# Two parts of down ahead of the first chunk in seven products, and the last half tile of the output in two pieces

## The chip, the cores and the metric

The kernel runs on one core of one Trainium2 chip. Its time is the device time of one execution in microseconds (us). Three runs of the kernel before took 1874.52 to 1875.6 us, with a median of 1874.64.

The engines are TensorE (PE; its weight loads are listed apart as PEld), VectorE (DVE), ScalarE (ACT), GpSimd (POOL) and SyncE (SP), which here issues the DMAs.

## The reference

A decoder of two layers on a sequence of 512 tokens of width 1024. Each layer has a feed-forward network (FFN), a mixer and another FFN, each behind an RMSNorm and added to x:

```python
def rmsnorm(x, g):
    y = x * lax.rsqrt(jnp.mean(x * x, axis=-1, keepdims=True) + EPS)
    return y * g

def swiglu(h, w_gate, w_up, w_down):
    return (jax.nn.silu(h @ w_gate) * (h @ w_up)) @ w_down

for i in range(2):
    x = x + 0.5 * swiglu(rmsnorm(x, ffn1_norm[i]), ffn1_w_gate[i], ...)
    x = x + mixer(rmsnorm(x, mix_norm[i]))     # i = 0: gated linear attention, i = 1: stick-breaking
    x = x + 0.5 * swiglu(rmsnorm(x, ffn2_norm[i]), ffn2_w_gate[i], ...)
return rmsnorm(x, final_norm)
```

w_gate and w_up are 1024 x 2816, w_down is 2816 x 1024, all float32. The change touches the four FFNs and the final norm; the mixers stay as they are.

## The kernel before, in words

**Split operands.** x lives in SBUF as eight tiles `xs[k]` of 128 features by 512 tokens, float32. TensorE multiplies in a float32 form with fewer bits, so each operand is cut into a high part (a cast) and a low part (operand minus high part), and each product is three matmuls: high by high, low by high, high by low (`mm3`, L67). For a weight, `Entry.split` (L108) does it: ScalarE casts (L124), VectorE subtracts (L126). Tiles `wh` and `wl` hold 1024 columns each and have four buffers; half-wide ones, `vh` and `vl`, have one. The loads themselves, issued by SyncE at L89, go to `raw` (1 MB of gate or up, two buffers) or `rawd` (512 KB of down, two buffers).

**The feed.** All of TensorE's work on weights stands in one list of entries, each with its weights and a body that issues its matmuls. When an entry starts (`Feed.start`, L137 on), the weights of up to three entries from it on are split, as long as no more than four units are needed, those up to four are viewed (a view may itself compute a sum of weights), and those up to six are loaded. The order of the entries is the order on TensorE. On the other engines a scheduler places the instructions after a model of their times, so one that is written later may stand earlier.

**An FFN** (class `FFN`). The 2816 hidden features are eleven chunks of 256 in six groups: chunks 0-1, 2-3, 4-5, 6-7, 8 and 9-10. For chunks 0 and 1, each half chunk of gate and of up is a feature entry (`feat`): 24 matmuls of 512 columns. The first six features take the input not yet normalized, while four pieces of `normed_input` (L615 among their lines) prepare the normalized one.

From chunk 2 on, gate and up come by `seven`: a 2 x 2 block product made from seven products instead of eight, by sums of weights (`s12`, `s34`; L506 to L513) and sums of inputs (`ts`, cut by L605 and L606 into `th` and `tl`). One chunk of gate or up is two entries. `body_1` has four of the products, `body_2` three; each is 12 matmuls of 256 columns at L523. `body_1` copies its first product to a second PSUM bank (L547) before its third product goes into the first bank. `body_2` begins with a product of the `s34` weights. Its results go through VectorE (L566, L569) and the gate (SiLU at L533, or the multiply at L536), and for an up chunk through `close`, which cuts the hidden features into `hh` and `hl`.

The eight cut sums of the input come from `sums`. The first five are spread over the entries that lie between the sixth and number `sums_by` of the FFN, the number at which the first chunk in seven products begins.

**Down** (L292). A group of four hidden features is multiplied by w_down in four parts, one entry each: two tiles of 128 output features, each 4 x 3 matmuls of 512 columns into one PSUM bank, then one VectorE operation that adds half of it to `xs[k]` (L307). The parts of a group's down are put between the entries of the next group. In entry order, with S for a chunk in seven products (two entries), g and u for gate and up and d0 to d3 for the parts of down of chunks 0 and 1:

```
8 features, S g2, d0, S u2, d1, S g3, d2, S u3, d3, S g4, ...
```

**The end.** In the last FFN, the last group's down is `back_tok` (L316): tokens on the partitions, 512 of the 1024 features in each of eight half tiles (i = 0..3 tokens, dh = 0, 1), 4 x 3 matmuls of 512 columns each. `last` (L1198) then adds half of it to x (L1201), squares and sums it (L1204), and for dh = 0 multiplies by the norm's gain (L1207). For dh = 1 it adds the two halves' sums (L1210), takes `rstd` (L377 to L388, seven small operations), scales both halves (L1212, L1214) and issues the two output DMAs (L1213, L1215).

Of the kernel before, what the change touches and what calls it, by code (L numbers as in the profile page):

```python
# [10 lines left out]
F32 = mybir.dt.float32  # L11
# [3 lines left out]
AF = mybir.ActivationFunctionType  # L15
ALU = mybir.AluOpType
PSUM = bass.MemoryType.PSUM

P = 128
T = 512  # L20
D = 1024
KD = D // P
FF = 2816
NT = T // P
EPS = 1e-6
# [7 lines left out]
def decoder(ctx: ExitStack, tc: tile.TileContext, a: dict, out: bass.AP):  # L33
    nc = tc.nc
# [6 lines left out]
    sp = ctx.enter_context(tc.tile_pool(name="sp", bufs=1))  # L41
# [5 lines left out]
    def psum(name, tag=None):  # L47
        if tag is None:
            tag = order[turn_[0] % 8]
            turn_[0] += 1  # L50
        return pp.tile([P, T], F32, tag=tag, bufs=banks[tag], name=name)
# [5 lines left out]
    gT = cp.tile([P, 51], F32, name="gT")  # L57
# [5 lines left out]
    def mm(ps, l, r, first, last):  # L63
        st["pe"] = nc.tensor.matmul(ps, l, r, start=first, stop=last).ins  # L64

    def mm3(ps, wh, wl, mh, ml, first, last):
        mm(ps, wh, mh, first, False)  # L67
        mm(ps, wl, mh, False, False)
        mm(ps, wh, ml, False, last)
# [219 lines left out]

                feed.q.append(Entry([u], body))  # L290

    def down(w, r0, nf, hs, part, nxt):  # L292

        nd = KD // nf
        src = w[r0 : r0 + nf * P, part * nd * P : (part + 1) * nd * P]
        ch = Chunk(src.rearrange("(f p) c -> p f c", p=P), nf, nd * P)
        ch.few = True

        def body(W):
            (wh, wl), = W  # L300
            for m in range(nd):
                ps = psum("ps_d")
                s = slice(m * P, (m + 1) * P)
                for f in range(nf):
                    mm3(ps, wh[:, f, s], wl[:, f, s], hs[f][0], hs[f][1], f == 0, f == nf - 1)
                k = part * nd + m
                nc.vector.scalar_tensor_tensor(  # L307
                    out=xs[k], in0=ps, scalar=0.5, in1=xs[k], op0=ALU.mult, op1=ALU.add
                )
                if nxt is not None:  # L310
                    nxt(k)
                yield

        feed.q.append(Entry([(ch, lambda t: t, nf, nd * P)], body))

    def back_tok(w, r0, nf, hs, done):  # L316

        units = []
        for dh in range(2):
            src = w[r0 : r0 + nf * P, dh * 512 : dh * 512 + 512]  # L320
            ch = Chunk(src.rearrange("(f p) c -> p f c", p=P), nf, 512)
            for u in range(0, nf, 2):
                units.append((ch, (lambda t, u=u: t[:, u : u + 2]), 2, 512))

        def body(W):
            for i in range(NT):
                s = slice(i * P, (i + 1) * P)
                for dh in range(2):
                    ps = psum("ps_bt")
                    for f in range(nf):  # L330
                        wh, wl = W[dh * (nf // 2) + f // 2]
                        hh, hl = hs[f]
                        mm(ps, hh[:, s], wh[:, f % 2], f == 0, False)
                        mm(ps, hh[:, s], wl[:, f % 2], False, False)
                        mm(ps, hl[:, s], wh[:, f % 2], False, f == nf - 1)
                    done(dh, i, ps)
            yield

        feed.q.append(Entry(units, body))


    st = {}
# [23 lines left out]
    def stats_a(tag=None):  # L366

        if st["ss"] is None:
            sums = st["sums"]
        else:  # L370
            ps = psum("ps_st", tag)
            for i in range(NT):
                mm(ps[:, i : i + 1], st["ss"][:, i * P : (i + 1) * P], ones[:, 0:1], True, True)
            sums = ps[:, 0:NT]
        st["r4"] = rstd(sums, NT)

    def rstd(sums, n):  # L377
        v = sp.tile([P, n], F32, tag="rv", bufs=2, name="rv")
# [56 lines left out]
    class FFN:  # L435
# [4 lines left out]


        GROUPS = ((0, 2), (2, 4), (4, 6), (6, 8), (8, 9), (9, 11))
        NORMED, SEVEN = 6, 2
        SEVEN_UP = (2, 3, 4, 5, 6, 7, 8, 9, 10)

        def __init__(self, wg, wu, wd, gi, nxt, first=False, last=False):
            self.gi, self.normed = gi, False
            self.defer, self.gates = [], []
            self.lead = []
            self.hs = [[] for _ in self.GROUPS]  # L450
            base, downs = len(feed.q), []
            self.sums_by = 10**6
            for group, (c0, c1) in enumerate(self.GROUPS):
                slots, put = 2 * (c1 - c0), 0
                for i in range(slots):
                    c, f = c0 + i // 2, i % 2
                    if f == 0:
                        g, u = Chunk(cols(wg, c * 256, 256), KD, 256), Chunk(cols(wu, c * 256, 256), KD, 256)
                    d = self.defer if i == 0 and c == 0 else None
                    f_ = f  # L460
                    if first and c == 0:

                        g, u = (Chunk(cols(w, f * P, P), KD, P) for w in (wg, wu))
                        self.lead += [g, u]
                        f_ = 0
                    if c >= self.SEVEN:
                        if f == 0:
                            self.sums_by = min(self.sums_by, len(feed.q) - base)
                            self.seven(g)
                    elif c not in self.SEVEN_UP:  # L470
                        feat(g, f_, self.evac_g, defer=d)
                    elif f == 0:
                        feat(g, 0, self.evac_g), feat(g, 1, self.evac_g)
                        self.sums_by = min(self.sums_by, len(feed.q) - base)
                    if c not in self.SEVEN_UP:
                        feat(u, f_, lambda ps, h=group: self.evac_u(ps, h), defer=d)
                    elif f == 1:
                        self.seven(u, group)

                    while c >= self.SEVEN and put < len(downs) * (i + 1) // slots:  # L480
                        down(*downs[put])
                        put += 1
                for x in downs[put:]:
                    down(*x)
                n = 2 * (c1 - c0)
                end = group + 1 == len(self.GROUPS)
                downs = [(wd, c0 * 256, n, self.hs[group], part, nxt if end else None) for part in range(n)]
            self.count = len(feed.q) - base
            if last:
                back_tok(wd, c0 * 256, n, self.hs[group], nxt)  # L490
            else:
                for x in downs:
                    down(*x)
            self.total = len(feed.q) - base
# [686 lines left out]
    xt = {}  # L1181

    def to_tokens(tp):
        fin = st["fin"] = tp.tile([P, D], F32, tag="s", bufs=4, name="fin")
        nc.gpsimd.dma_start(fin, a["final_norm"].partition_broadcast(P))

        for hf in range(2):
            ps = [psum("ps_T") for _ in range(NT)]
            for m in range(4):
                for i in range(NT):  # L1190
                    nc.tensor.transpose(
                        ps[i][:, m * P : (m + 1) * P], xs[hf * 4 + m][:, i * P : (i + 1) * P], ident
                    )
            for i in range(NT):
                xt[i, hf] = xs[hf * 4 + i]
                nc.scalar.copy(xt[i, hf], ps[i])

    def last(dh, i, ps):  # L1198

        x = xt[i, dh]  # L1200
        nc.vector.scalar_tensor_tensor(out=x, in0=ps, scalar=0.5, in1=x, op0=ALU.mult, op1=ALU.add)  # L1201
        fin = st["fin"]
        sq = st["sq"][:, 2 * i + dh : 2 * i + dh + 1]
        nc.scalar.activation(ps, x, AF.Square, accum_out=sq)  # L1204
        rows = out[0, i * P : (i + 1) * P]
        if dh == 0:
            nc.vector.tensor_tensor(out=x, in0=x, in1=fin[:, 0:T], op=ALU.mult)  # L1207
            return
        s = st["sq"][:, 2 * i : 2 * i + 1]
        nc.vector.tensor_tensor(out=s, in0=s, in1=sq, op=ALU.add)  # L1210
        r = rstd(s, 1)
        nc.vector.scalar_tensor_tensor(out=x, in0=x, scalar=r, in1=fin[:, T:D], op0=ALU.mult, op1=ALU.mult)  # L1212
        nc.sync.dma_start(rows[:, T:D], x)  # L1213
        nc.scalar.activation(xt[i, 0], xt[i, 0], AF.Copy, scale=r)  # L1214
        nc.sync.dma_start(rows[:, 0:T], xt[i, 0])  # L1215

    ffn(1, 0, 0, lambda k: prep(k, 2), first=True)
    phases.append(
# [9 lines left out]
    with tc.tile_pool(name="ip", bufs=1) as ip:  # L1228
# [9 lines left out]
        sums = [ip.tile([P, NT], F32, name=f"sums{hf}") for hf in range(2)]  # L1238
# [8 lines left out]
        ps = psum("ps_g")  # L1247
# [34 lines left out]
    for ph in phases[:-1]:  # L1282
        ph.run()

    st["sq"] = gT[:, 0 : 2 * NT]
    phases[-1].run(between=to_tokens)


# [38 lines left out]
```

## Time and profile before

| what | value |
|---|---|
| median of three runs | 1874.64 us |
| the profiled execution | 1874.33 us |
| its span, first to last instruction | 1872.2 us |
| TensorE busy | 1847.3 us, 99% of the span |
| VectorE busy | 1412.0 us, 75% |
| ScalarE busy | 1012.5 us, 54% |
| DMA | 95 GB/s over the span |
| last matmul starts / span ends | 1864.08 / 1872.2 us |

A line of the profile's groups reads: source line, engine, operation, out<-in, partitions x elements and type, count | busy us in total, mean ns of one | idle us of the engine just before them, and what ended it. A line of a timeline reads: start in us from the span's start, duration, engine, line, operation; in brackets the idle time before it and its releaser. Durations of neighbouring instructions on an engine overlap a little, so the distance between starts says what one costs in a row.

### The profile page before, as it was taken

The page shows a single profiled execution, that of the slowest core. Times are in us where ns is not written, and L with a number is a line of the kernel's source. Part 1 is how long each engine was busy: PE and PEld are TensorE (multiplying, and loading weights), DVE is VectorE, ACT ScalarE, POOL GpSimd, SP SyncE. Part 2 cuts the span into 40 slices and gives each one's busy share as a digit, 9 for nine tenths or more (in the row PEclk, how much of TensorE's full clock was granted, in tenths as well). Part 3 has the DMA queues.
Part 4 walks back from the last instruction along what each step waited for, and adds up shares of the span by engine and source line. Part 5 has one row for each costly group of instructions (what it writes and reads, how often), then busy time and mean ns, then how long its engine had stood idle before and what let it go on. Part 6 is the DMA issues. An engine that isn't in the chain of part 4 may idle for free.

```text
span 1872.2 us, 29140 instructions
## 1 busy us (share of the span) xinstructions
PE 1847.3 (99%) x11933; PEld 1650.8 (88%) x11933; DVE 1412.0 (75%) x2177; ACT 1012.5 (54%) x1714; POOL 7.3 (0%) x17
## 2 busy tenths in 40 slices
PE   8999999999999999999999999999999999999998
PEld 6899999789888899999888999998888788999997
DVE  7977776775767987777788777676878769777775
ACT  6544545444555554454555545445878755554454
POOL 0000000100000000000000000000000000000000
PEclk9999999999999999999999999999999999999999
DMA  5433333212123233342233333233221223333321
GB/s 158 130 107 110 105 113 103 87 48 66 61 75 113 79 102 102 107 129 80 79 113 116 111 102 113 79 92 101 68 68 57 68 90 113 102 102 102 119 85 68
DMA packets 177513, 179.04 MB, mean 96 GB/s; under 512 B 4034, under 2 KB 167924, under 8 KB 177380
## 3 DMA queue, kind: packets, MB, share of 16 engines
q1 hardware_dynamic: 176768, 176.18, 30.0%
q8 instruction: 93, 1.52, 0.3%
q0 software_dynamic: 512, 0.99, 0.2%
q14 instruction: 40, 0.33, 0.1%
q10 hardware_dynamic: 100, 0.03, 0.0%
HBM read 175.11 MB, written 2.10 MB: 95 GB/s over the span
## 4 chain that ended last, share of the span: by engine, by line
PE 88%; DVE 9%; ACT 1%; issue 1%; DMA 0%; SPq 0%; DVEq 0%; ACTq 0%
PE ps_d L64 25%; PE ps_w L523 20%; PE ps_f L64 11%; PE ps_q L523 10%; PE ps_z L523 5%; PE ps_t L64 5%; PE ps_b L64 4%; DVE wl L126 2%; PE ps_S L64 1%; PE ps_z L1058 1%; PE ps_bt L64 1%; DVE ts L615 1%; DVE xn L599 1%; DVE nl L606 1%; PE ps_oT L1120 1%; PE ps_T L1105 1%
## 5 line engine op out<-in xcount | busy, mean ns | idle before, releaser
L126 DVE TENSOR_TENSOR wl<-raw,wh 128x1024 fp32r<-128x1024 f32 x244 | 259.9, 1066 | 96.6 <-ACT wh L124 61.5
L124 ACT CAST wh<-raw 128x1024 fp32r<-128x1024 f32 x244 | 224.7, 923 | 131.2 <-PE ps_f L64 44.4
L64 PE MATMUL ps_d<-hh,wl 128*128 128x512 f32 x672 | 262.4, 390 | 0.0
L64 PE MATMUL ps_d<-hh,wh 128*128 128x512 f32 x672 | 262.3, 390 | 0.0
L64 PE MATMUL ps_d<-hl,wh 128*128 128x512 f32 x672 | 261.6, 389 | 0.0
L523 PE MATMUL ps_w<-th,wl 128*128 128x256 f32 x864 | 239.1, 277 | 5.0 <-DVE wl L126 5.0
L523 PE MATMUL ps_w<-tl,wh 128*128 128x256 f32 x864 | 239.0, 277 | 0.9 <-DVE tl L606 0.9
L523 PE MATMUL ps_w<-th,wh 128*128 128x256 f32 x864 | 239.2, 277 | 0.2
L307 DVE SCALAR_TENSOR_TENSOR x<-ps_d,x 128x512 f32<-128x512 f32 x184 | 124.9, 689 | 115.9 <-PE ps_d L64 115.6
L126 DVE TENSOR_TENSOR wl<-s,wh 128x1024 fp32r<-128x1024 f32 x144 | 176.1, 1223 | 40.7 <-PE ps_z L523 19.3
L124 ACT CAST wh<-s 128x1024 fp32r<-128x1024 f32 x144 | 151.2, 1050 | 93.2 <-PE ps_q L523 30.0
L124 ACT CAST wh<-rawd 128x1024 fp32r<-128x1024 f32 x84 | 88.4, 1053 | 201.7 <-issue 98.9
L64 PE MATMUL ps_f<-xh,wh 128*128 128x512 f32 x448 | 182.1, 407 | 1.6 <-DVE q L721 1.5
L64 PE MATMUL ps_f<-xl,wh 128*128 128x512 f32 x448 | 175.5, 392 | 0.0
L64 PE MATMUL ps_f<-xh,wl 128*128 128x512 f32 x448 | 175.0, 391 | 0.0
L523 PEld LDWEIGHTS ps_w<-th,wl 128*128 128x128 f32 x864 | 162.3, 188 | 5.8 <-DVE wl L126 5.8
L523 PEld LDWEIGHTS ps_w<-tl,wh 128*128 128x128 f32 x864 | 162.2, 188 | 1.1 <-DVE tl L606 1.1
L523 PEld LDWEIGHTS ps_w<-th,wh 128*128 128x128 f32 x864 | 162.2, 188 | 1.0 <-ACT wh L124 1.0
L64 PEld LDWEIGHTS ps_d<-hl,wh 128*128 128x128 f32 x672 | 126.2, 188 | 26.7
L64 PEld LDWEIGHTS ps_d<-hh,wh 128*128 128x128 f32 x672 | 126.2, 188 | 24.5
L64 PEld LDWEIGHTS ps_d<-hh,wl 128*128 128x128 f32 x672 | 126.2, 188 | 23.8
L126 DVE TENSOR_TENSOR wl<-rawd,wh 128x1024 fp32r<-128x1024 f32 x84 | 102.9, 1225 | 53.6 <-ACT wh L124 40.1
(248 smaller groups left out, 4434.4 us busy)
## 6 DMA issues: line engine op xcount, KB each, us to landing
raw<-in_ffn_w_gate_dram SPq DMA_DIRECT2D x43, 1024.0 KB, 5.3
raw<-in_ffn_w_up_dram SPq DMA_DIRECT2D x43, 1024.0 KB, 5.4
rawd<-in_ffn_w_down_dram SPq DMA_DIRECT2D x84, 512.0 KB, 3.5
raw<-in_gla_w_in_dram SPq DMA_DIRECT2D x12, 1024.0 KB, 5.5
raw<-in_sb_w_in_dram SPq DMA_DIRECT2D x16, 512.0 KB, 3.8
raw<-in_gla_w_out_dram SPq DMA_DIRECT2D x4, 1024.0 KB, 5.0
raw<-in_sb_w_in_dram SPq DMA_DIRECT2D x4, 1024.0 KB, 5.3
raw<-in_sb_w_out_dram SPq DMA_DIRECT2D x4, 1024.0 KB, 5.0
```

What stands on the lines that cost most here:

```text
L64: st["pe"] = nc.tensor.matmul(ps, l, r, start=first, stop=last).ins
L124: st["cut"] = nc.scalar.copy(h, r).ins
L126: nc.vector.tensor_tensor(out=l, in0=r, in1=h.bitcast(F32), op=ALU.subtract)
L307: nc.vector.scalar_tensor_tensor(out=xs[k], in0=ps, scalar=0.5, in1=xs[k], op0=ALU.mult, op1=ALU.add)
L523: st["pe"] = nc.tensor.matmul(o, l_, r_, start=first and j + n == 0, stop=j == 3 and n == 2, skip_group_check=True).ins
L599: nc.vector.scalar_tensor_tensor(out=t, in0=xs[k], scalar=g, in1=st["R"], op0=ALU.mult, op1=ALU.mult)
L606: nc.vector.tensor_tensor(out=l, in0=t, in1=h.bitcast(F32), op=ALU.subtract)
L615: nc.vector.tensor_tensor(out=o, in0=p, in1=q, op=ALU.subtract)
L1058: nc.tensor.matmul(o_, l_, r_, start=first, stop=last, skip_group_check=True)
L1105: nc.tensor.transpose(ps[:, c0 : c0 + P], ys[yb][:, yc + j * P : yc + (j + 1) * P], ident)
L1120: nc.tensor.matmul(po[e * 64 : e * 64 + 64, j * P : T], self.v[j][:, c : c + 64], self.wt[p, e][bk][:, c0 : c0 + n], start=j == 0, stop=j ...
```

## The change

In each FFN, when the second group begins, two of the four parts of down for chunks 0 and 1 are put ahead of the first chunk in seven products. The entry order becomes

```
8 features, d0, d1, S g2, S u2, S g3, d2, S u3, d3, S g4, ...
```

`sums_by` counts the entries ahead of the first chunk in seven and so goes from 8 to 10: the first five cut sums are spread over four entries instead of two. d0 gets `late=1`: both its tiles take their first three features before either takes the fourth, so two PSUM banks are open at once.

In `back_tok`, the last half tile (i = 3, dh = 1) is computed in two pieces of 256 columns, each with its own 12 matmuls and PSUM bank. `last` adds and squares each piece by itself. While the second piece is squared, the sums of the earlier ones are added up. A new `rstd_1` takes the earlier sum as a scalar operand and joins two of `rstd`'s multiplies into one operation, by working with the sum instead of the mean; it is used for all four token tiles. The product with the gain goes into a new tile `xf` instead of x.

```diff
-    def down(w, r0, nf, hs, part, nxt):
+    def down(w, r0, nf, hs, part, nxt, late=0):
...
+            acc = []
+
+            def prod(m, fs):
+                if m == len(acc):
+                    acc.append(psum("ps_d"))
+                s = slice(m * P, (m + 1) * P)
+                for f in fs:
+                    mm3(acc[m], wh[:, f, s], wl[:, f, s], hs[f][0], hs[f][1], f == 0, f == nf - 1)
+
+            if late:
+                for m in range(nd):
+                    prod(m, range(nf - late))
             for m in range(nd):
-                ps = psum("ps_d")
-                s = slice(m * P, (m + 1) * P)
-                for f in range(nf):
-                    mm3(ps, wh[:, f, s], wl[:, f, s], hs[f][0], hs[f][1], f == 0, f == nf - 1)
+                prod(m, range(nf - late if late else 0, nf))
+                ps = acc[m]
...
     def back_tok(w, r0, nf, hs, done):
...
-                    ps = psum("ps_bt")
-                    for f in range(nf):
...
-                    done(dh, i, ps)
+                    cuts = (0, 256, 512) if (i, dh) == (NT - 1, 1) else (0, 512)
+                    for c0, c1 in zip(cuts, cuts[1:]):
+                        ps = psum("ps_bt")[:, 0 : c1 - c0]
+                        c = slice(c0, c1)
+                        for f in range(nf):
...
+                        done(dh, i, ps, c0, c1)
...
+    def rstd_1(sums, more):
+
+        v = sp.tile([P, 1], F32, tag="rv", bufs=2, name="rv")
+        nc.vector.tensor_scalar(out=v, in0=sums, scalar1=more, scalar2=D * EPS, op0=ALU.add, op1=ALU.add)
+        y = sp.tile([P, 1], F32, tag="ry", bufs=2, name="ry")
+        nc.scalar.activation(y, v, AF.Sqrt)
+        nc.vector.reciprocal(y, y)
+        q = sp.tile([P, 1], F32, tag="rq", bufs=2, name="rq")
+        nc.vector.scalar_tensor_tensor(out=q, in0=y, scalar=v, in1=y, op0=ALU.mult, op1=ALU.mult)
+        c = float(D) ** 0.5
+        nc.vector.tensor_scalar(out=q, in0=q, scalar1=-0.5 * c, scalar2=1.5 * c, op0=ALU.mult, op1=ALU.add)
+        r = sp.tile([P, 1], F32, tag="r4", bufs=2, name="r1")
+        nc.vector.tensor_tensor(out=r, in0=y, in1=q, op=ALU.mult)
+        return r
...
-        NORMED, SEVEN = 6, 2
+        NORMED, SEVEN, AHEAD = 6, 2, 2
...
+                if group == 1:
+
+                    for put in range(self.AHEAD):
+                        down(*downs[put], late=put == 0)
+                    put = self.AHEAD
...
-    def last(dh, i, ps):
+    def last(dh, i, ps, c0, c1):
+
+        x, fin = xt[i, dh], st["fin"]
+        c = slice(c0, c1)
+        nc.vector.scalar_tensor_tensor(out=x[:, c], in0=ps, scalar=0.5, in1=x[:, c], op0=ALU.mult, op1=ALU.add)
+        if c0 == 0:
+            n = 2 * i + dh
+        else:
+
+            n = 2 * NT
+            s = st["sq"][:, n - 2 : n - 1]
+            nc.vector.tensor_tensor(out=s, in0=s, in1=st["sq"][:, n - 1 : n], op=ALU.add)
+        sq = st["sq"][:, n : n + 1]
+        nc.scalar.activation(ps, x[:, c], AF.Square, accum_out=sq)
         if dh == 0:
-            nc.vector.tensor_tensor(out=x, in0=x, in1=fin[:, 0:T], op=ALU.mult)
-            return
...
+            st["xf"] = st["tp"].tile([P, T], F32, tag="s", bufs=4, name="xf")
+            nc.vector.tensor_tensor(out=st["xf"], in0=x, in1=fin[:, 0:T], op=ALU.mult)
+        elif c1 == T:
+            rows = out[0, i * P : (i + 1) * P]
+            r = rstd_1(sq, st["sq"][:, 2 * i : 2 * i + 1])
...
```

More of the change, by code (lines that the diff above doesn't have):

```diff
@@ L328, in body @@
                 for dh in range(2):
-                    ps = psum("ps_bt")
-                    for f in range(nf):
[L331 to L335, printed above, removed]
-                    done(dh, i, ps)
+                    cuts = (0, 256, 512) if (i, dh) == (NT - 1, 1) else (0, 512)
[3 more added lines that the diff above has]
+                        for f in range(nf):
+                            wh, wl = W[dh * (nf // 2) + f // 2]
+                            hh, hl = hs[f]
+                            mm(ps, hh[:, s], wh[:, f % 2, c], f == 0, False)
+                            mm(ps, hh[:, s], wl[:, f % 2, c], False, False)
+                            mm(ps, hl[:, s], wh[:, f % 2, c], False, f == nf - 1)
+                        done(dh, i, ps, c0, c1)
             yield
@@ L1183, in to_tokens @@
     def to_tokens(tp):
+        st["tp"] = tp
         fin = st["fin"] = tp.tile([P, D], F32, tag="s", bufs=4, name="fin")
@@ L1196, in to_tokens @@
                 nc.scalar.copy(xt[i, hf], ps[i])
-    def last(dh, i, ps):
[L1200 to L1205, printed above, removed]
-        if dh == 0:
-            nc.vector.tensor_tensor(out=x, in0=x, in1=fin[:, 0:T], op=ALU.mult)
-            return
[L1209 to L1215, printed above, removed]
+    def last(dh, i, ps, c0, c1):
[10 more added lines that the diff above has]
+        nc.scalar.activation(ps, x[:, c], AF.Square, accum_out=sq)
+        if dh == 0:
+            st["xf"] = st["tp"].tile([P, T], F32, tag="s", bufs=4, name="xf")
[3 more added lines that the diff above has]
+            r = rstd_1(sq, st["sq"][:, 2 * i : 2 * i + 1])
+            nc.vector.scalar_tensor_tensor(out=x, in0=x, scalar=r, in1=fin[:, T:D], op0=ALU.mult, op1=ALU.mult)
+            nc.sync.dma_start(rows[:, T:D], x)
+            nc.scalar.activation(st["xf"], st["xf"], AF.Copy, scale=r)
+            nc.sync.dma_start(rows[:, 0:T], st["xf"])
     ffn(1, 0, 0, lambda k: prep(k, 2), first=True)
@@ L1283, in decoder @@
         ph.run()
-    st["sq"] = gT[:, 0 : 2 * NT]
+    st["sq"] = gT[:, 0 : 2 * NT + 1]
     phases[-1].run(between=to_tokens)
```

## The prediction

> **What bounds the kernel now.** I read the page's busy shares, the clock row and the chain by engine first, then TensorE's list of waits, then a table of stretches around the first chunk in seven products, then the timeline there and at the end.
>
> ```profile
> span 1872.2 us, 29140 instructions
> PE 1847.3 (99%) x11933; PEld 1650.8 (88%) x11933; DVE 1412.0 (75%) x2177; ACT 1012.5 (54%) x1714; POOL 7.3 (0%) x17
> ...
> PEclk9999999999999999999999999999999999999999
> ...
> PE 88%; DVE 9%; ACT 1%; issue 1%; DMA 0%; SPq 0%; DVEq 0%; ACTq 0%
> ```
>
> TensorE is busy 99% of the span at full granted clock, and the change takes no product away. Only TensorE's idle time and the tail behind its last matmul can be won. The chain's 9% on DVE says which engine it then waits for.
>
> ```profile
> PE ps_w L523 <- DVE wl L126: 5.0, 4, 1.4
> PE ps_w L523 <- DVE tl L606: 0.9, 1, 0.9
> ```
>
> Columns: engine and tile, releaser, total us, times, longest. Four waits for a weight's low part on VectorE, one in each FFN, and one for the low part of a sum. The idle records hold only 5.9 us; the next view shows what they cost (length, then busy us of PE, PEld, DVE, ACT, POOL).
>
> ```profile
> 38.00:60.37 22.37, 22.37 (x100) 18.52 (x99) 22.37 (x39) 13.85 (x22) 0.00 (x0) 1.00 0.29 94
> 60.37:72.00 11.63, 10.21 (x85) 9.81 (x84) 11.63 (x17) 6.46 (x11) 0.00 (x0) 1.00 0.45 135
> 72.00:77.47 5.47, 5.47 (x26) 4.51 (x25) 5.47 (x10) 2.50 (x5) 0.00 (x0) 1.00 0.38 103
> 77.47:86.99 9.52, 9.52 (x85) 9.52 (x84) 9.01 (x15) 5.78 (x9) 0.00 (x0) 1.00 0.34 108
> ...
> 92.46:101.98 9.52, 9.52 (x86) 9.52 (x84) 7.64 (x11) 6.11 (x11) 0.00 (x0) 1.00 0.38 128
> 643.08:655.38 12.30, 10.44 (x86) 9.85 (x84) 12.28 (x18) 6.55 (x11) 0.00 (x0) 1.00 0.41 128
> 982.72:994.22 11.50, 10.08 (x85) 9.69 (x84) 11.50 (x17) 6.46 (x11) 0.00 (x0) 1.00 0.44 136
> 1567.31:1578.80 11.49, 10.08 (x85) 9.68 (x84) 11.49 (x17) 6.45 (x11) 0.00 (x0) 1.00 0.43 137
> 1789.97:1809.01 19.04, 19.04 (x169) 19.03 (x168) 10.99 (x16) 11.99 (x21) 0.53 (x1) 1.00 0.18 57
> ```
>
> A chunk in seven products is 84 matmuls of 256 columns. Undisturbed (77.47:86.99) it takes 9.52 us, and two of them back to back (1789.97:1809.01) take 19.04. The first one of each FFN takes 11.63, 12.30, 11.50 and 11.49: 2.11, 2.78, 1.98 and 1.97 more, **8.84 us in all**. VectorE is full in all four, and was full all the way from 38.00 to 60.37: a backlog, not one slow instruction. One part of down (72.00:77.47) is 24 matmuls in 5.47 us.
>
> ```profile
> 60.37 0.28 PE L523 MATMUL ps_w<-nh,w 128*128 128x256 f32 x1
> ...
> 66.50 1.23 DVE L126 TENSOR_TENSOR wl<-s,wh 128x1024 fp32r<-128x1024 f32 x1
> 67.63 1.23 DVE L126 TENSOR_TENSOR wl<-rawd,wh 128x1024 fp32r<-128x1024 f32 x1
> ...
> 67.78 0.38 PE L523 MATMUL ps_w<-th,wl 128*128 128x256 f32 x1 [1.37 <-DVE wl L126]
> ...
> 72.00 0.40 PE L64 MATMUL ps_d<-hh,wh 128*128 128x512 f32 x1
> ```
>
> The fifth of the seven products opens the chunk's second entry. Four of seven, 48 matmuls at 9.52/84 = 0.113 us, bring TensorE there at 60.37 + 5.44 = 65.81. The low part that it needs begins at 66.50 and the matmul goes at 67.78. Successive starts on VectorE (66.50, 67.63) set a 1024-element subtract at 1.13 us.
>
> **The change, part by part.**
>
> *The stall.* Two parts of down, 2 x 5.47 = 10.94 us of TensorE work, move ahead of the first chunk in seven. That entry's second half is needed at 60.37 + 10.94 + 5.44 = 76.75.
>
> ```profile
> 51.64 1.25 DVE L126 TENSOR_TENSOR wl<-raw,wh 128x1024 fp32r<-128x1024 f32 x1
> ```
>
> ```profile
> L126 DVE TENSOR_TENSOR wl<-rawd,wh 128x1024 fp32r<-128x1024 f32 x84 | 102.9, 1225 | 53.6 <-ACT wh L124 40.1 <-PE ps_z L523 13.4
> L307 DVE SCALAR_TENSOR_TENSOR x<-ps_d,x 128x512 f32<-128x512 f32 x184 | 124.9, 689 | 115.9 <-PE ps_d L64 115.6
> ```
>
> What comes onto VectorE with them is two splits (2 x 1.13) and four evictions. A 512-element operation is listed at 0.69 with starts about 0.60 apart, so 2.26 + 2.40 = 4.66 us, against 10.94 us more time. I walked VectorE's new order from the instruction at 51.64, from which on the two kernels' orders differ, at these pitches: that subtract ends its pitch at 52.77; three 512-wide operations, 54.6; first down weight, 55.7; third feature's low part, **56.3**; a sum's low part, second down weight, two halves of a weight sum with a low part between, 59.9; gate 2's first low part, 61.0; the fourth feature's product (it waits for the last feature, 60.37 + 0.20), 61.6; another weight, 62.7; its low part, **63.3**; two sums and a half weight, 65.1; two evictions, each as TensorE ends its tile, 66.6; two sums and three steps for coming weights, 69.6; an eviction, 70.2; then the low part that stalled TensorE, **71.4** against 76.75; a weight step, the last eviction, two weight steps and the last sum's low part, **74.4** against 76.75. They have 5.4 and 2.4 us to spare. So the stall goes in FFN 1, and in the others, whose stretches have the same queue and a VectorE as full. FFN 2's is 0.7 us deeper, which the 2.4 cover. What is early can't give more than the stall. **-8.84.**
>
> What is late next? The moved part itself: it needs the low part of the group's third feature at 60.37 and of the fourth 18 matmuls in (18 x 5.47/24 = 4.10), at 64.47. The first part of down is split for this: both its tiles take three features before either takes the fourth. In the walk the third is there at 56.3, the fourth at 63.3: 1.2 us to spare, 0.5 if all of FFN 2's 0.7 falls here. The weights are split by 55.7. I cost it at 0; with its cover gone it stalls by at most what the fourth's lateness would be, bounded by one 1024 subtract, 1.13 us per FFN.
>
> *Three chunks in a row.* The parts of down no longer stand between chunks 2 gate, 2 up and 3 gate, so 28.56 us of seven products run together; before shows only two in a row. VectorE's work in them, by the up chunk at 77.47:86.99 and the gate at 92.46:101.98, is 7.64 + 9.01 + 7.64 = 24.3 us, so it isn't full. The tight place is the start of the third, on ScalarE.
>
> ```profile
> L124 ACT CAST wh<-raw 128x512 fp32r<-128x512 f32 x72 | 44.0, 612 | 1.2 <-PE ps_w L523 1.2
> L605 ACT CAST hh<-o 128x512 fp32r<-128x512 f32 x72 | 44.4, 622 | 42.6 <-DVE o L536 42.6
> L547 ACT COPY ps_z<-ps_w 128x256 f32<-128x256 f32 x72 | 25.7, 357 | 10.4 <-PE ps_w L523 6.7
> L569 DVE TENSOR_TENSOR o<-ps_q,o 128x256 f32<-128x256 f32 x72 | 30.2, 419 | 0.0
> ```
>
> TensorE's third product there overwrites the bank that L547 copies, so it waits for the copy, 2 x 1.36 = 2.72 us after the chunk's start. Ahead of the copy on ScalarE stand one weight cast and the two casts that close the up chunk; behind it wait the second copy and the split for the next chunk. A weight's cast can begin when the up chunk's last product ends, then 3 x about 0.52 and the copy's 0.36 with its hand-overs: ready 2.1 us after the start, 0.6 to spare. Bounds: 0, and the whole queue late by one cast of a 1024 weight, 0.95 - 0.6 = 0.35 us, or by its transfer, below. I take 0, the nearer row being the pair without a stall. SyncE issues the same loads; the first two down weights stood ahead of gate 2's load before too, and the third and fourth (0.5 MB each) now go ahead of gate 3's load, at about 55.7 and 58.0 as the first two are split, and no longer behind it. Nothing wants their share then: gate 3's buffer comes free only near 69. POOL's queue has nothing in it here.
>
> *The tail.* Behind the last matmul:
>
> ```profile
> 1864.08 0.39 PE L64 MATMUL ps_bt<-wh,hl 128*128 128x512 f32 x1
> 1864.51 0.69 DVE L1201 SCALAR_TENSOR_TENSOR x<-ps_bt,x 128x512 f32<-128x512 f32 x1 [0.20 <-PE ps_bt L64]
> 1865.29 0.60 ACT L1204 ACTIVATE ps_bt<-x 128x512 f32<-128x512 f32 x1 [1.71 <-DVE x L1201]
> ...
> 1866.05 0.16 DVE L1210 TENSOR_TENSOR gT<-gT 128x1 f32<-128x1 f32 x1 [0.85 <-ACT ps_bt L1204]
> 1866.24 0.15 DVE L379 TENSOR_SCALAR rv<-gT 128x1 f32<-128x1 f32 x1
> ...
> 1867.06 0.16 DVE L385 TENSOR_TENSOR rq<-rq,rv 128x1 f32<-128x1 f32 x1
> 1867.25 0.15 DVE L386 TENSOR_SCALAR rq<-rq 128x1 f32<-128x1 f32 x1
> ```
>
> Adding only the last 256 columns saves 0.69 - 0.42 = 0.27 (the 256-wide row L569); squaring them 0.60 - 0.36 = 0.24 (256 wide, L547). The sum at L1210 needs only earlier columns and goes while ScalarE squares: 1866.24 - 1866.05 = 0.19. L384 and L385 become one: 1867.25 - 1867.06 = 0.19. Together **-0.89**. The halved tile has 24 matmuls of 256 columns for 12 of 512: 24 x 0.113 against 12 x 0.228, no difference, and the first half's 0.4 + 0.4 us on VectorE and ScalarE end before the second half's last matmul. Bounds: -1.1 to 0.
>
> The Trainium skill ("TensorE: Matmul & The Clock Gate", "LDWEIGHTS (loading the stationary operand)" and "The mechanism") puts a 128-column weight load at about 107 ns and says that it overlaps a running matmul only where the row groups differ; by this, as an estimate, the halving's 12 more loads would cost 1.3 us and turn the tail into +0.4. The stretch 77.47:86.99, with a load for each 256-column matmul and no idle time, speaks against it.
>
> *Sum:* -8.84 - 0.89 = -9.73. The profiled execution took 1874.33 (1872.2 of span and 2.1 around it), 0.31 under the median of the runs, 1874.64. So 1864.60 for it, **1864.9** for the median.
>
> **The rivals.**
>
> *Crowding.* The third chunk in a row, or the fourth feature, stalls a little in each FFN. ScalarE's queue there also holds a cast from the chunk 3 up weight.
>
> ```profile
> raw<-in_ffn_w_up_dram SPq DMA_DIRECT2D x43, 1024.0 KB, 5.4
> ```
>
> Its buffer comes free about 1.8 to 2.1 us into the up chunk, so at 5.4 us it lands at 7.2 to 7.5, just where ScalarE would copy the fifth product (6.8 + 0.2). Each further 0.6 us of lateness uses up the margin above, then stalls one for one. 0.5 to 1.0 us four times gives 1866.9 to 1868.9. For it: no row shows three in a row. Against: 0.6 us to spare at the median landing.
>
> *The stall only moves.* The gap repeats at one place in all four FFNs; if it were a shortage of weight buffers (four of each kind), the second entry's split would still wait for a buffer after the move, and only the tail's 0.89 would be won: 1873.8. Against: the four windows show VectorE without an idle moment, so the subtract waited in a queue, not for a buffer. The Trainium skill ("Perfetto Trace Analysis", "Optimization Strategy") says that a gap that keeps repeating on the busy engine can mean too little room for the next tile. By that rule this rival holds; the rows name VectorE.
>
> *Slower.* One mechanism: the chunk 3 up load lands late, ScalarE stands in order behind its cast, the copies of the up chunk and so its gates, closes and L547 come late, and TensorE stands. To undo 9.73 us and add 0.2% takes 13.5 us, 3.4 per FFN, so a landing past 5.4 + 0.6 + 3.4 = 9.4 us in all four: 1878.4 or more. Against: the mean landing of 43 such loads, and DMA at 29% to 45% in these windows.
>
> **How the numbers follow.** Forecast 0.72, crowding 0.14, stall moved 0.07, slower 0.07. The likeliest is 1864.9. The range goes from 1863.9 (a tail, and hand-overs, better by some 0.2 each with the 0.6 scatter of the runs) to 1869.0 (crowding's end): 0.86 less the edges. A measurement of this kernel tells about 0.2% from no change, 3.7 us. Forecast and crowding are faster by more than this: 0.86; stall moved is within it: 0.07; slower 0.07.
>
> **What would show it.** Right: the first chunk in seven of each FFN at 9.52 us, the waits for wl L126 and tl L606 gone from TensorE's list, VectorE no longer full between the two parts of down, L1210's work beside the last square, and 0.8 to 1.0 us less from last matmul to end. Wrong: a new wait on ACT ps_z or on DVE hl, a stretch of three chunks over 28.6 us, or the same wait for wl at a later place.

## The result, and the profile after

The changed kernel takes 1867.18 us (median of five runs, 1866.19 to 1867.66) against 1874.64 (five runs, 1874.13 to 1876.18): 0.9958 of the time before, 95% interval 0.9946 to 0.9969. It is 7.5 us faster. The forecast was 9.7 us, 1864.9; the range (1863.9 to 1869.0) holds the result. The profiled execution took 1867.25 us with a span of 1865.3.

The page of the changed kernel, its busy shares and its chain by engine:

```profile
span 1865.3 us, 29157 instructions
PE 1845.7 (99%) x11945; PEld 1650.8 (88%) x11945; DVE 1409.8 (76%) x2171; ACT 1009.2 (54%) x1708; POOL 7.3 (0%) x17
...
PE 95%; DVE 2%; DMA 1%; ACT 1%; issue 0%; ACTq 0%; DVEq 0%; SPq 0%
```

VectorE's part of the chain fell from 9% to 2%: in TensorE's list of waits, the two for VectorE in the seven products (wl L126 and tl L606) are gone. In their place stands one for ScalarE (engine and tile, releaser, total us, times, longest):

```profile
PE ps_w L558 <- ACT u L600: 1.0, 1, 1.0
```

The stretches of the changed kernel, in each FFN the first chunk in seven products (2 gate) and the one behind it (2 up); the columns are those of the prediction's table, L558 is L523 of before:

```profile
71.14:80.66 9.52, 9.52 (x86) 9.52 (x84) 9.52 (x15) 5.92 (x10) 0.00 (x0) 1.00 0.28 96
80.66:90.18 9.52, 9.52 (x87) 9.52 (x85) 5.87 (x10) 6.07 (x12) 0.00 (x0) 1.00 0.33 110
651.78:661.30 9.52, 9.52 (x85) 9.51 (x84) 9.52 (x15) 5.85 (x9) 0.00 (x0) 1.00 0.30 104
661.30:671.13 9.83, 9.79 (x86) 9.59 (x85) 6.50 (x10) 6.24 (x12) 0.00 (x0) 1.00 0.33 107
988.91:998.43 9.52, 9.52 (x85) 9.52 (x84) 9.52 (x15) 5.91 (x10) 0.00 (x0) 1.00 0.28 95
998.43:1009.24 10.81, 9.84 (x86) 9.64 (x85) 6.21 (x10) 5.97 (x12) 0.00 (x0) 1.00 0.32 99
1009.24:1019.13 9.89, 9.89 (x86) 9.89 (x85) 9.48 (x16) 6.52 (x12) 0.00 (x0) 1.00 0.48 161
1573.61:1583.13 9.52, 9.52 (x85) 9.52 (x84) 9.39 (x15) 5.91 (x10) 0.00 (x0) 1.00 0.28 97
1583.13:1592.88 9.75, 9.75 (x87) 9.62 (x85) 6.32 (x10) 6.14 (x12) 0.00 (x0) 1.00 0.35 110
```

All four first chunks take 9.52 us: the 8.84 us of stall are gone, as forecast. But the chunk behind takes 0.31, 1.29 and 0.23 us too long in FFNs 2, 3 and 4, and in FFN 3 the third chunk 0.37. That is 2.20 us given back; FFN 1 loses nothing. The list above holds only the longest of these stalls, FFN 3's; the stretches show all of them.

ScalarE's and TensorE's timelines at the worst place, FFN 3:

```profile
1007.11 0.30 ACT L131 CAST w<-raw 128x128 fp32r<-128x128 f32 x1 [1.98 <-DMA raw<-in_ffn_w_up_dram]
1007.31 0.36 ACT L600 COPY u<-ps_w 128x256 f32<-128x256 f32 x1
```

```profile
1006.48 0.28 PE L558 MATMUL ps_q<-nl,wh 128*128 128x256 f32 x1
1007.73 0.39 PE L558 MATMUL ps_w<-th,wh 128*128 128x256 f32 x1 [0.97 <-ACT u L600]
```

ScalarE stands 1.98 us in front of an instruction that the chunk doesn't need: the lead copy (L131), a copy of the first 128 columns of the weight of chunk 3 up, which waits for that weight's load. Behind it in ScalarE's order stands the copy of the fifth product (L600). The seventh product goes into the bank that this copy reads, so TensorE waits for it.

Where the 6.93 us of span between the two profiled executions come from, by the times at which equal matmuls start: FFNs 1 to 4 gave 2.14, 2.56, 0.37 and 1.79 (6.86); the last half tile and the end 0.55; the start 0.14; the mixers, whose instructions did not change, took back 0.15 and 0.47.

### The profile page after: what moved, and what is told of

The parts are those of the page before. It is cut to its first block, busy times and chain, and to the rows that moved or that the text cites. A ratio compares the mean times of both kernels' runs of the same rounds, so it can differ in the third digit from the quotient of the medians.

```text
span 1865.3 us, 29157 instructions
## 1 busy us (share of the span) xinstructions
PE 1845.7 (99%) x11945; PEld 1650.8 (88%) x11945; DVE 1409.8 (76%) x2171; ACT 1009.2 (54%) x1708; POOL 7.3 (0%) x17
## 4 chain that ended last, share of the span: by engine, by line
PE 95%; DVE 2%; DMA 1%; ACT 1%; issue 0%; ACTq 0%; DVEq 0%; SPq 0%
PE ps_d L64 25%; PE ps_w L558 21%; PE ps_f L64 18%; PE ps_q L558 10%; PE ps_z L558 5%; PE ps_t L64 5%; PE ps_b L64 4%; PE ps_S L64 1%; PE ps_z L1093 1%; PE ps_bt L64 1%; PE ps_oT L1155 1%; PE ps_T L1140 1%; PE ps_o L64 1%; DMA raw<-in_ffn_w_up_dram 1%; DVE wl L126 0%; PE ps_R L431 0%
## 5 line engine op out<-in xcount | busy, mean ns | idle before, releaser
L126 DVE TENSOR_TENSOR wl<-raw,wh 128x1024 fp32r<-128x1024 f32 (+1 forms) x244 | 259.2, 1064 | 92.2 <-ACT wh L124 63.1
L124 ACT CAST wh<-raw 128x1024 fp32r<-128x1024 f32 (+1 forms) x244 | 224.8, 923 | 142.2 <-PE ps_f L64 44.3
L558 PE MATMUL ps_w<-th,wh 128*128 128x256 f32 x864 | 238.9, 276 | 1.0 <-ACT u L600 1.0
L558 PE MATMUL ps_w<-tl,wh 128*128 128x256 f32 x864 | 238.6, 276 | 0.0
L558 PE MATMUL ps_w<-th,wl 128*128 128x256 f32 x864 | 238.6, 276 | 0.0
L126 DVE TENSOR_TENSOR wl<-s,wh 128x1024 fp32r<-128x1024 f32 x144 | 175.8, 1222 | 52.4 <-ACT wh L124 26.4
L558 PEld LDWEIGHTS ps_w<-th,wh 128*128 128x128 f32 x864 | 162.2, 188 | 1.5 <-ACT u L600 1.4
L558 PEld LDWEIGHTS ps_w<-tl,wh 128*128 128x128 f32 x864 | 162.2, 188 | 0.0
L558 PEld LDWEIGHTS ps_w<-th,wl 128*128 128x128 f32 x864 | 162.2, 188 | 0.0
L126 DVE TENSOR_TENSOR wl<-rawd,wh 128x1024 fp32r<-128x1024 f32 x84 | 102.8, 1224 | 51.6 <-ACT wh L124 38.1
```

What stands on the lines that cost most here:

```text
L124: st["cut"] = nc.scalar.copy(h, r).ins
L126: nc.vector.tensor_tensor(out=l, in0=r, in1=h.bitcast(F32), op=ALU.subtract)
L558: st["pe"] = nc.tensor.matmul(o, l_, r_, start=first and j + n == 0, stop=j == 3 and n == 2, skip_group_check=True).ins
```

## The experiments

The theory: the stall went because the two parts of down give VectorE time, and what came back is the lead copy that holds ScalarE's queue until its load lands. Rivals: ScalarE or VectorE is late by its own work; the stall went because the sums are spread; the tail's weight loads cost something.

Each ratio is taken against runs of the kernel before that stand beside it: 1873.97 us for the tail alone, no lead copy, one part ahead and d0 in plain order, 1874.67 for the other four. Differences of under 1 us between the two sets are therefore read from the traces, not from the medians.

**Only the tail.**

```diff
-        NORMED, SEVEN, AHEAD = 6, 2, 2
+        NORMED, SEVEN, AHEAD = 6, 2, 0
```

> Only the tail of the change; the parts of down stay where they were (AHEAD = 0, so d0 isn't split either). My account: the tail is worth 0.8 to 0.9 us and the four stalls of 1.98 to 2.78 us stay, so about 1873.8 us, and the first chunk in seven of each FFN takes 11.5 to 12.3 us as before. Rival (the last tile's extra weight loads cost 1.3 us): 1875.0.

Measured: 1873.7 us (ten runs) against 1873.97, ratio 0.9998 (0.9988 to 1.0007): too little to see in the times. TensorE's list of waits has the old stalls:

```profile
PE ps_w L558 <- DVE wl L126: 4.9, 4, 1.3
...
PE ps_w L558 <- DVE tl L641: 0.9, 1, 0.9
```

From the last half tile's first matmul to the end it is 10.10 us in this trace, 10.11 in the changed kernel's, 10.66 before: the tail is worth 0.55, less than the 0.8 to 0.9 expected, and the rival's added 1.3 us is not there.

**No lead copy for chunk 3 up.**

```diff
-                        self.seven(u, group)
+                        self.seven(u, group, lead=c != 3)
...
-            lead = feed.q[-1].place != NEAR
+            lead = lead and feed.q[-1].place != NEAR
```

> The change, but the up weight of chunk 3 gets no lead copy (the 128 columns that ScalarE copies ahead, L131); its first matmul takes its weights from the split tile. In the changed kernel TensorE stood 0.31, 1.29 and 0.23 us in the up chunk of chunk 2 in FFNs 2, 3 and 4, waiting for ScalarE's copy of the fifth product, which stood behind this lead copy, which waited for the load. Theory (the load lands too late and the lead copy holds ScalarE's queue): all three stalls go, and with FFN 3's also the slower pace of 118 ns a matmul behind it (0.37 us): 1.8 to 2.2 us less, about 1865.1, with the three chunks in a row at 28.56 us in every FFN. Rival (ScalarE or VectorE is late by its own work, whatever the load does): the stalls stay, 1867.2.

Measured: 1866.42 us (1866.25 to 1866.86), ratio 0.996 (0.9945 to 0.9974). No wait for ACT u is left in the list, and the three chunks in a row take 9.52 us each in every FFN. But the chunk that lost its lead copy runs at 118 ns a matmul in all four FFNs, against 113 for the one before it, which has no lead copy either but follows a chunk directly:

```profile
104.76:114.65 9.89, 9.89 (x85) 9.89 (x84) 8.46 (x14) 5.58 (x8) 0.00 (x0) 1.00 0.34 114
89.78:99.30 9.52, 9.52 (x87) 9.52 (x86) 9.23 (x16) 6.11 (x12) 0.00 (x0) 1.00 0.52 167
```

So, in the traces, 2.20 us came back and 4 x 0.37 = 1.48 were paid for it. By the rival the stalls would have stayed; they went. My 1865.1 missed the price of going without the lead copy.

**The lead copy behind the copy that it held.**

```diff
-                nc.scalar.copy(u3, w)
+                st["u3"] = nc.scalar.copy(u3, w).ins
...
-                        nc.scalar.copy(first, r[:, 0])
+                        with tc.issue_after(st["u3"]) if "u3" in st else ExitStack():
+                            nc.scalar.copy(first, r[:, 0])
```

> The change with one instruction moved: the lead copy of a chunk's first weight (on ScalarE) may not stand ahead of the latest copy of a fifth product (L600 in the changed kernel). On ScalarE this swaps the two once in each FFN, in the up chunk of chunk 2, and nothing else. Theory (that lead copy waits for its load and holds the copy behind it): the stalls of 0.31, 1.29 and 0.23 us and the slower pace behind the second (0.37) go, and unlike without any lead copy all chunks keep 113 ns a matmul: 9.52 us each, about 1865.0 us. Rival (the copy is late for another reason): 1867.2, and TensorE still waits for ACT u.

Measured: 1865.43 us (1864.26 to 1865.67), ratio 0.9951 (0.9934 to 0.9968). ScalarE's timeline at the same place in FFN 3:

```profile
1004.70 0.37 ACT L601 COPY u<-ps_w 128x256 f32<-128x256 f32 x1 [0.36 <-PE ps_w L559]
1005.76 0.30 ACT L132 CAST w<-raw 128x128 fp32r<-128x128 f32 x1 [0.69 <-DMA raw<-in_ffn_w_up_dram]
1006.01 1.06 ACT L124 CAST wh<-rawd 128x1024 fp32r<-128x1024 f32 x1
```

The same two instructions, swapped. The load is late here too: the lead copy waits 0.69 us for it and starts 8.1 us after its chunk's start, later than in FFNs 2 and 4 of the changed kernel (7.75 and 7.63), which stalled. But nothing that TensorE needs stands behind it now, and no chunk of the four FFNs stalls. This settles the cause: it takes the late load and the order on ScalarE together.

**The load twice.**

```diff
                 nc.sync.dma_start(self.t, self.src)
+                if self.twice:
+                    nc.sync.dma_start(self.t, self.src)
...
+                    u.twice = c == 3
```

> The change, with the up weight of chunk 3 loaded twice one after the other, so that it lands about 5.3 us later; the result is the same. The scheduler then places its lead copy later, behind the copy of the fifth product and ahead of the copy of chunk 3 gate's first product (ps_z). Theory: the stalls at the seventh product go, and a new one of the same kind comes at the third product of chunk 3 gate: landing at 2.0 + 5.4 + 5.3 = 12.7 us after the up chunk's start, the two copies end near 13.4, wanted at 9.52 + 2.72 = 12.24: 1.2 us in each FFN, or 4.8 in all with perhaps 0.25 of slower pace each, so 1865.0 + 4.8 to 5.8 = about 1870. Rival (the load's landing has no part in it): 1867.2.

Measured: 1871.7 us (ten runs, 1870.7 to 1872.97), ratio 0.9984 (0.9975 to 0.9993). The wait went where it was expected:

```profile
PE ps_w L562 <- ACT ps_z L586: 5.2, 4, 1.9
```

```profile
1015.61 0.30 ACT L134 CAST w<-raw 128x128 fp32r<-128x128 f32 x1 [2.80 <-DMA raw<-in_ffn_w_up_dram]
1015.81 0.37 ACT L586 COPY ps_z<-ps_w 128x256 f32<-128x256 f32 x1
```

The chunk 3 gate takes 10.84, 11.13, 11.67 and 11.27 us, 1.32 to 2.15 too long and 6.83 in all: more than the 4.8 to 5.8 expected, mainly since the loads landed later than assumed, again most in FFN 3. In this place too the lead copy held what stood behind it.

**All four parts ahead.**

```diff
-        NORMED, SEVEN, AHEAD = 6, 2, 2
+        NORMED, SEVEN, AHEAD = 6, 2, 4
```

> All four parts of down ahead of the first chunk in seven, so four of them run in a row and none has a lead copy but the first. Theory (the lead copy behind the up weight's load holds ScalarE): no lead copy of chunk 3's up weight, so no stall at the seventh product, and as a chunk follows a chunk directly the pace stays 113 ns: about 1865.0. VectorE's and ScalarE's work in the four chunks (2 x 7.64 + 2 x 9.01 = 33.3 of 38.1 us) leaves room. Rival (a longer row of chunks starves TensorE of split weights): over 38.1 us for the four, 1867 to 1871.

Measured: 1869.64 us (eight runs), ratio 0.9972 (0.9962 to 0.9983): slower than two ahead, and in the trace the chunks lose 3.50 us, for 2.20 there. My expectation was wrong. I had counted four chunks in a row. With no part of down left, 4 gate follows 3 up directly, so it is five, and the next lead copy is that of chunk 4 up. It does in chunk 3 up what the other did in chunk 2 up; the two lines are FFN 1's:

```profile
118.61 0.30 ACT L131 CAST w<-raw 128x128 fp32r<-128x128 f32 x1 [1.30 <-DMA raw<-in_ffn_w_up_dram]
118.82 0.37 ACT L600 COPY u<-ps_w 128x256 f32<-128x256 f32 x1
```

```profile
PE ps_w L558 <- ACT u L600: 1.1, 3, 0.6
...
PE ps_w L558 <- ACT ps_z L582: 0.8, 1, 0.8
```

**One part ahead.**

```diff
-        NORMED, SEVEN, AHEAD = 6, 2, 2
+        NORMED, SEVEN, AHEAD = 6, 2, 1
```

> The change with one part of down ahead instead of two, so two chunks in a row (2 gate, 2 up), then the second part, then 3 gate. A part moved ahead gives 5.47 us and brings VectorE 1.13 + 2 x 0.60 = 2.33 us of work, 3.14 net. My account: the subtract that stalled TensorE by 2 us has 5.4 - 3.1 = 2.3 us to spare, the last cut sum is 2.4 - 3.1 = 0.7 late but wanted about 1 us into its product, so nearly all of the old stall is gone (0 to 0.7 us an FFN stays); and gate 3's load, which now has a lead copy, goes early enough. 1865 to 1867.5. Rival (the second part's time is needed too): half of the stall stays, 1870 or more.

Measured: 1864.75 us (1864.52 to 1865.01), ratio 0.995 (0.9935 to 0.9965), the fastest median here and a little under the range expected. The first chunk of each FFN:

```profile
65.89:75.41 9.52, 9.52 (x85) 9.52 (x84) 9.52 (x13) 6.73 (x11) 0.00 (x0) 1.00 0.37 112
...
646.72:656.24 9.52, 9.52 (x85) 9.51 (x84) 9.52 (x13) 6.74 (x11) 0.00 (x0) 1.00 0.35 113
983.56:993.08 9.52, 9.52 (x85) 9.51 (x84) 9.52 (x13) 6.73 (x11) 0.00 (x0) 1.00 0.34 112
1566.05:1575.57 9.52, 9.52 (x86) 9.52 (x84) 9.52 (x13) 6.74 (x11) 0.00 (x0) 1.00 0.35 112
```

VectorE is full in all four, but it is no longer late. One part removes the whole stall, in FFN 2 too, and no other chunk stalls in this trace. Against the kernel before beside it, it gains 9.2 us, and so do two parts with the lead copy held back. So the second part bought nothing, and by making the row of chunks three long it brought the lead copy to the wrong place.

**d0 in plain order.**

```diff
-                        down(*downs[put], late=put == 0)
+                        down(*downs[put])
```

> The change, but the first part of down takes all four features of a tile in order (late = 0). My account from the changed kernel's trace in FFN 1: the fourth feature's low part is done at 63.3 us and would be used at 60.26 + 11 x 0.228 = 62.8, so TensorE waits 0.5 to 0.7 us in each FFN: 2.0 to 2.8 us more, about 1869.6. Rival (the split of d0 does nothing, because the low part is early enough): 1867.2.

Measured: 1865.93 us (1865.85 to 1866.63), ratio 0.9958 (0.9941 to 0.9974): not slower, and no wait of a down matmul for VectorE. The reason lies in the order on TensorE: the scheduler itself puts four matmuls of the second tile between those of the first tile's fourth feature. So this edit did not undo what it was meant to undo, and whether the split of d0 is needed without that stays open. FFN 3 (0.81) and FFN 4 (0.21) still stalled at the lead copy, less than in the changed kernel's trace: that loss goes with the load and varies from run to run.

**The sums as early as before.**

```diff
-                spread(todo[:5], self.sums_by - self.NORMED)
+                spread(todo[:5], 2)
+                feed.entries(self.sums_by - self.NORMED - 2)
```

> The change, with the first five cut sums spread over the last two features as before, not over four entries. It tells whether the stall went because the two parts of down give time, or because the sums come later. My account: VectorE has the same work ahead of the subtract that stalled TensorE and 5.4 us to spare; the third and fourth feature's low parts come up to 1.2 us later, of which the fourth has 1.5 to spare, so no or a short stall in d0: 1866.5 to 1868.5. Rival (the spreading is what removed the stall): the four stalls of about 2 us are back, 1874.

Measured: 1866.41 us (1866.18 to 1866.8), ratio 0.9956 (0.9941 to 0.9971). The old stalls did not come back; only FFN 3's wait for the lead copy shows:

```profile
PE ps_w L558 <- ACT u L600: 0.8, 1, 0.8
```

It is the time that the parts of down give, not the spreading.

## Why the prediction was right, and where it was not

**The bound and the stall: right.** The walk of VectorE's order had the subtract that stalled TensorE end at 71.4 and the last sum at 74.4. The changed kernel's timeline of VectorE:

```profile
55.61 0.69 DVE L641 TENSOR_TENSOR hl<-t,hh 128x512 fp32r<-128x512 f32 x1
...
62.69 0.69 DVE L641 TENSOR_TENSOR hl<-t,hh 128x512 fp32r<-128x512 f32 x1
...
70.19 1.22 DVE L126 TENSOR_TENSOR wl<-s,wh 128x1024 fp32r<-128x1024 f32 x1
...
73.73 0.69 DVE L641 TENSOR_TENSOR tl<-ts,th 128x512 fp32r<-128x512 f32 x1
```

By the starts of what follows they end at 71.33 and 74.34; the third and fourth features' low parts, put at 56.3 and 63.3, at 56.21 and 63.29. The -8.84 was right as a sum of stalls removed, and so was the 0 for the moved part itself. One sign did not come: VectorE was to be no longer full between the two parts of down, and it is full there, 10.84 of 10.88 us. It had been given later work earlier; full and late are not the same.

```profile
60.26:71.14 10.88, 10.88 (x50) 9.01 (x48) 10.84 (x16) 2.72 (x3) 0.00 (x0) 1.00 0.15 42
```

**Three chunks in a row: wrong.** This is the step that failed: "I take 0, the nearer row being the pair without a stall." The trace gave back 2.20 us there, and the prediction's sign of being wrong was seen: the three chunks take 28.87, 30.22 and 28.79 us in FFNs 2 to 4, over 28.6. The rival called crowding, at 0.14, is what happened, and the result lies between its 1866.9 and 1868.9; its 0.5 to 1.0 us four times over is not what the trace shows, for 1.66 of the 2.20 fell in FFN 3. The range holds the result because it was drawn to hold this rival. Two things were missed. I put the tight place at L547's copy in the third chunk, with 0.6 us to spare. It is three products earlier, in the second chunk: the seventh product overwrites the bank of the fifth, so the fifth's copy must be done at six products, 6 x 1.36 = 8.16 us. And I knew that the load would land "just where ScalarE would copy the fifth product", and the rival called slower had the mechanism, ScalarE standing in order behind that weight's cast; but I counted the 0.6 us of the other place as reserve here too. From the lead copy's start to TensorE's start is 0.62 us (1007.11 to 1007.73), so the load may land at 7.5 at the latest. The lead copies of FFNs 1, 2 and 4, beside FFN 3's above:

```profile
87.87 0.30 ACT L131 CAST w<-raw 128x128 fp32r<-128x128 f32 x1 [0.52 <-DMA raw<-in_ffn_w_up_dram]
669.05 0.30 ACT L131 CAST w<-raw 128x128 fp32r<-128x128 f32 x1 [1.05 <-DMA raw<-in_ffn_w_up_dram]
1590.76 0.30 ACT L131 CAST w<-raw 128x128 fp32r<-128x128 f32 x1 [0.94 <-DMA raw<-in_ffn_w_up_dram]
```

In the order of the FFNs they start 7.21, 7.75, 8.68 and 7.63 us after their chunk's start: FFN 1 in time, the others late by 0.1 to 1.1, about 0.1 less than TensorE lost. The runs with d0 in plain order and with early sums divide at the same place: no chunk lost whose lead copy started at 7.13 to 7.34 us, and those at 7.62, 8.24 and 8.52 did. In FFNs 2 and 4 the load took the median 5.4 us but was issued at 2.35 and 2.23 us, in FFN 3 it was issued at 2.01 and took 6.6. My own 7.2 to 7.5 us for the median landing left 0 to 0.3 us of reserve, not 0.6.

**The slower pace: not in the sum.** 0.37 us in FFN 3, behind the stall.

**The tail: right in kind, 0.55 for 0.89.** From the last matmul's start to the end it is 0.81 us less (7.36 for 8.17), as the sign asked, but the halved tile starts that matmul 0.26 us later than before. The last half tile takes 2.87 us on TensorE for 2.72 (the stretch up to the end of its last pitch, after and before):

```profile
1855.21:1858.08 2.87, 2.87 (x25) 2.82 (x23) 2.65 (x6) 1.47 (x4) 0.00 (x0) 1.00 0.33 126
```

```profile
1861.59:1864.31 2.72, 2.72 (x13) 2.06 (x11) 2.43 (x6) 1.38 (x3) 0.00 (x0) 1.00 0.20 74
```

24 matmuls at 120 ns, not at the 113 that I took from the seven products: 0.15. Another 0.12 is in two of the small operations behind:

```profile
1859.34 0.21 DVE L395 TENSOR_SCALAR rv<-gT 128x1 f32<-128x1 f32 x1 [0.57 <-ACT ps_bt L1247]
...
1860.02 0.22 DVE L400 SCALAR_TENSOR_TENSOR rq<-ry,rv 128x1 f32<-128x1 f32 x1
1860.27 0.15 DVE L402 TENSOR_SCALAR rq<-rq 128x1 f32<-128x1 f32 x1
```

The first two take a column as their scalar, and each costs 0.06 us more than the form that it replaces (0.15 and 0.16 before). The last 0.07 is spread over the square of 256 columns (0.39 us where I took 0.36) and the steps up to the output. The Trainium skill's rule ("TensorE: Matmul & The Clock Gate", "LDWEIGHTS (loading the stationary operand)" and "The mechanism"), by which as an estimate the 12 added weight loads would cost 1.3 us, does not fit this trace: the whole halving cost 0.15. The second of these sections also names another case, a load into a background weight buffer, which goes ahead of running matmuls; no run here shows which case holds, only that the loads were all but hidden.

**The rivals.** The stall did not move to another wait on VectorE, so it was no shortage of buffers. The slower case asked for landings past 9.4 us in all four FFNs; with the load issued twice the lead copies started 10.5 to 11.6 us after the first issue, and it took 1871.7, not 1878.4, since the scheduler then placed them behind the copy of the fifth product. One part ahead and the held lead copy each gain 9.2 us against the kernel before beside them, where I had 9.7: for a kernel without the lead copy's wait the sum was 0.5 too high, 0.34 of it the tail.

## What to carry to other kernels

Where an engine runs in order, ask of each instruction that waits for a transfer what stands behind it: a small copy that was needed 17 us later held a copy that was needed at once. When a stall comes from a backlog, move just enough work ahead to clear it; one part cleared all of it here, and the second only made a longer row without pauses, in which loads came late. And follow each bank from its reader to its next writer over the whole stretch: the tightest one was not where I looked.

## What the runs showed of the hardware that was not expected

- Behind some stalls, and where a chunk without a lead copy follows 512-column matmuls, the 256-column matmuls keep a pace of 118 ns, not 113, with the granted clock at 1.00. In the changed kernel's FFN 3 it held for the whole next chunk (9.89 us) and ended with the 512-column matmuls behind it. It did not follow every stall: after those of FFN 2 and FFN 4 in the same kernel the pace was 113, and in the kernel before it was 118 behind the stalls of FFNs 1 and 2, 113 behind those of 3 and 4. Why is open.
- One load of 1 MB landed 5.2 us after its issue in FFN 1 and 6.6 us in FFN 3, with nothing else on the queue. The changed kernel's transfers from 998.4 to 1009 us, in 40 slices, show a tail of 1.6 us at 23 GB/s behind the 360, and most of ScalarE's 1.98 us of waiting is that tail. What made it is open:

```profile
GB/s 31 0 0 0 0 0 0 0 0 0 0 46 131 58 158 298 356 437 371 359 363 363 383 371 186 23 23 23 23 23 23 0 0 0 0 0 0 0 0 0
...
raw<-in_ffn_w_up_dram SPq DMA_DIRECT2D x1, 1024.0 KB, 6.6
```
